# Batched A·Bᵀ in fp32: products in column halves, stores of pairs in 16 KB runs, and one fixed order of transfers on the sync queue

## The chip, the cores and the metric

One core of one Trainium2 chip. The metric is the device time of one execution in microseconds, taken as the median of several runs. Each run has a state. All runs quoted here were in the fast state, and fast runs alone are compared. In each batch of experiments the kernel before ran on the same chip as well. Its medians over the batches were 124.9 to 125.2 us, so ratios are worth more here than differences between medians of different batches. A difference of two ratios is called shown below only where their 95% intervals are clear of each other.

## The reference

```python
batch, m, k, n = 16, 512, 512, 512          # a: [16, 512, 512], b: [16, 512, 512], fp32
def reference(a, b):
    return np.matmul(a, b.transpose(0, 2, 1)).astype(np.float32)
```

33.55 MB are read and 16.78 MB are written. The kernel casts to bf16 and accumulates in fp32.

## The kernel before

The matrices are taken in pairs, u = 0 to 7. A load brings two matrices (2 MiB, 16 KB per partition) into one of seven slots. VectorE casts them to bf16, TensorE transposes them against an identity, ScalarE and VectorE copy the transposed slices out of PSUM, TensorE multiplies, and ScalarE moves the products into one of seven output slots. These are the parts that the change touches (cuts marked):

```python
load(0, nc.scalar)                      # loads: ScalarE's queue (one on the sync queue)
load(1, nc.sync)
for n in range(2, NL): load(n, nc.scalar)
...
nc.sync.wait_ge(s_ld[0], 32)            # stores: the sync queue, after the eighth load
for n in range(batch - 1): store(n)     # 1 MiB, 8 KB per partition
...
for u in range(pairs):                  # ScalarE, unrolled
    for ko in range(KO):
        nc.scalar.wait_ge(s_ta, KO * u + ko + 1)
        for e in range(2):              # two copies of 128x512, sorted by matrix
            c = nc.scalar.copy(out=ta[:, ko, ...], in_=tp[:, ko % 2, ...])
        c.then_inc(s_ea, 1)
    for n in (2 * u + NL, 2 * u + NL + 1):
        if n < 2 * pairs: load(n, nc.scalar)
    ...                                 # 8 copies ob <- ps
...
for e in range(2):                      # TensorE: matrix e of the pair
    ...
    t = nc.tensor.matmul(ps[:, j, :],
            ta[:, ko, (e * J + j) * P:(e * J + j + 1) * P],      # 128 columns
            tb[:, ko, :]...[:, :, e * HP:(e + 1) * HP], ...)     # 512 columns stream
```

Of the kernel before, what the change touches and what calls it, by code (L numbers as in the profile page):

```python
# [10 lines left out]
def kernel(  # L11
# [6 lines left out]
    nc = tc.nc  # L18
    P = 128
    batch, M, K = a.shape  # L20
    _, N, _ = b.shape
    J = M // P
    KO = K // P
    HP = P // 2
    HK = K // 2
    pairs = batch // 2
    f32 = mybir.dt.float32
    bf16 = mybir.dt.bfloat16
    NL = 7
    NO = 7  # L30



    def sbuf(name, shape, dtype):
        return ctx.enter_context(nc.sbuf_tensor(name, shape, dtype))

    def sem(name):
        return tc.alloc_semaphore(name)

    with tc.tile_critical(no_gpsimd_drain=True):  # L40
# [5 lines left out]
        )  # L46
        ta = sbuf("ta", [P, KO, 2 * J * P], bf16)
        tb = sbuf("tb", [P, KO, 2 * J * P], bf16)
        ob = sbuf("ob", [P, NO, J, N], f32)
        tp = ctx.enter_context(nc.psum_tensor("tp", [P, 4, 2 * J, P], bf16))  # L50
        ps = ctx.enter_context(nc.psum_tensor("ps", [P, 4, N], f32))

        s_set = sem("s_set")
        s_ld = [sem(f"s_ld{i}") for i in range(NL)]
        s_st = [sem(f"s_st{i}") for i in range(NO)]

        s_go = sem("s_go")
        s_wa = sem("s_wa")
        s_wb = sem("s_wb")
        s_ca = sem("s_ca")  # L60
# [2 lines left out]
        s_ta = sem("s_ta")  # L63
        s_tb = sem("s_tb")
        s_ea = sem("s_ea")
        s_eb = sem("s_eb")
        s_mm = sem("s_mm")
        s_pv = sem("s_pv")
        s_out = sem("s_out")
# [12 lines left out]
        def load(n, engine):  # L82
            u, slot = n // 2, n % NL
            src = (a if n % 2 == 0 else b)[2 * u:2 * u + 2].rearrange(
                "e (p j) k -> (e p) j k", j=2 * J
            )
            engine.dma_start(ld[:, slot], src).then_inc(s_ld[slot], 16)

        def landed(n):
            return s_st[n % NO], 16 * (n // NO + 1)  # L90

        def store(n):
            nc.sync.wait_ge(s_out, n + 1)
            nc.sync.dma_start(
                out[n].rearrange("(p j) n -> p j n", j=J), ob[:, n % NO]
            ).then_inc(landed(n)[0], 16)

        load(0, nc.scalar)
        load(1, nc.sync)
        for n in range(2, NL):  # L100
            load(n, nc.scalar)

        for n in range(2 * pairs):
            nc.gpsimd.wait_ge(s_ld[n % NL], 16 * (n // NL + 1)).then_inc(s_go, 1)  # L104

        nc.sync.wait_ge(s_ld[0], 32)
        for n in range(batch - 1):
            store(n)

        def taker(engine):  # L110
            return lambda s, n: engine.wait_ge(s, n).then_inc(s, -n)  # L111
# [5 lines left out]
        take = taker(nc.vector)  # L117
# [3 lines left out]
        with nc.Fori(0, pairs, engines=[dve]) as u:  # L121
            for x, (h, w, s_c, s_w) in enumerate(
                ((ha, wa, s_ca, s_wa), (hb, wb, s_cb, s_wb))
            ):
                src = ld[:, bass.ds((u * 2 + x) % NL, 1)].rearrange("p o j k -> p (o j) k")
                take(s_go, 1)
                if x == 0:
                    take(s_da, 1)

                nc.vector.tensor_copy(out=h[:, :J, :], in_=src[:, :J, :HK])  # L130
                nc.vector.tensor_copy(  # L131
                    out=h[:, J:, :], in_=src[:, J:, :HK]
                ).then_inc(s_c, 1)
                nc.vector.tensor_copy(out=w[:], in_=src[:, :, HK:]).then_inc(s_w, 1)  # L134
            for ko in range(KO):
                if ko == 0:
                    take(s_wa, 1)
                    take(s_da, 1)
                    nc.vector.tensor_copy(out=ha[:], in_=wa[:]).then_inc(s_ca, 1)  # L139
                take(s_tb, 1)  # L140
                if ko == 1:
                    take(s_wb, 1)
                    nc.vector.tensor_copy(out=hb[:], in_=wb[:]).then_inc(s_cb, 1)  # L143
                nc.vector.tensor_copy(  # L144
                    out=tb[:, ko, :],
                    in_=tp[:, 2 + ko % 2].rearrange("k j p -> k (j p)"),
                ).then_inc(s_eb, 1)


        act = nc.scalar.engine  # L150
        nc.scalar.nop().then_inc(s_ea, 2)
        nc.scalar.copy(out=one[:], in_=nc.const_aps.tensor(1.0, (P, 1), f32))  # L152
        for u in range(pairs):
            for ko in range(KO):
                nc.scalar.wait_ge(s_ta, KO * u + ko + 1)
                for e in range(2):
                    c = nc.scalar.copy(  # L157
                        out=ta[:, ko, e * J * P:(e + 1) * J * P].rearrange(
                            "k (j p h) -> k j p h", j=J, h=2
                        ),  # L160
                        in_=tp[:, ko % 2, :, e * HP:(e + 1) * HP].rearrange(
                            "k (h j) p -> k j p h", h=2
                        ),
                    )
                c.then_inc(s_ea, 1)


            for n in (2 * u + NL, 2 * u + NL + 1):
                if n < 2 * pairs:
                    load(n, nc.scalar)  # L170
            for e in range(2):
                n = 2 * u + e
                if n >= NO:
                    nc.scalar.wait_ge(*landed(n - NO))
                for j in range(J):
                    nc.scalar.wait_ge(s_mm, J * n + j + 1)
                    c = nc.scalar.copy(  # L177
                        out=ob[:, n % NO, j, :].rearrange("m (p j) -> m p j", j=2 * J),
                        in_=ps[:, j, :].rearrange("m (j p) -> m p j", j=2 * J),
                    )  # L180
                    if e == 0:
                        c.then_inc(s_pv, 1)
                    elif j in (0, J - 1):
                        c.then_inc(s_out, 1)
# [3 lines left out]
        take = taker(nc.tensor)  # L188
        with nc.Fori(0, pairs, engines=[pe]):
            with nc.Fori(0, 2, engines=[pe]):  # L190

                for x, (h, s_c, s_t, s_e) in enumerate(
                    ((ha, s_ca, s_ta, s_ea), (hb, s_cb, s_tb, s_eb))
                ):
                    take(s_c, 1)
                    for g in range(2):
                        take(s_e, 1)
                        for j in range(2 * J):
                            t = nc.tensor.transpose(  # L199
                                tp[:, 2 * x + g, j, :], h[:, j, g * P:(g + 1) * P], ident[:]  # L200
                            )
                            if x == 1 and g == 0 and j == 0:
                                t.then_inc(s_da, 1)
                        t.then_inc(s_t, 1)



            for e in range(2):
                for jj in range(0, J, 2):
                    if e == 1:  # L210
                        take(s_pv, 2)
                    for kk in range(0, KO, 2):
                        for j in (jj, jj + 1):
                            for ko in (kk, kk + 1):
                                if (e, jj, j) == (0, 0, 0) and ko >= 2:
                                    nc.tensor.wait_ge(s_ea, ko - 1)
                                    nc.tensor.wait_ge(s_eb, ko - 1)
                                t = nc.tensor.matmul(  # L218
                                    ps[:, j, :],
                                    ta[:, ko, (e * J + j) * P:(e * J + j + 1) * P],  # L220
                                    tb[:, ko, :].rearrange("k (j p) -> k j p", j=2 * J)[
                                        :, :, e * HP:(e + 1) * HP
                                    ],
                                    start=(ko == 0),
                                    stop=(ko == KO - 1),
                                )
                            if kk == KO - 2:
                                t.then_inc(s_mm, 1)



    with tc.tile_critical(sync_engine=act, no_gpsimd_drain=True):
        for n in range(batch - NO, batch - 1):
            nc.scalar.wait_ge(*landed(n))
    waits = nc.cur_bb.bb.instructions[-1]
    last = nc.sync.dma_start(
        out[batch - 1].rearrange("(p j) n -> p j n", j=J), ob[:, (batch - 1) % NO]
    )
    tc.add_manual_dep(
        last.ins,  # L240
        waits.name,
# [33 lines left out]
```

## Time and profile before

| | before |
|---|---|
| median (fast runs) | 124.92 us |
| span of the profiled run | 123.1 us |
| TensorE, VectorE, ScalarE busy | 73%, 55%, 55% |
| two transfer queues, share of 16 engines' span | 60.6% + 36.4% |
| last load used, last product stored from PSUM | 100.41 us, 113.80 us |

The lines behind this table, and what follows from them, stand in the prediction below.

One more reading is used in this document. Each transfer leaves 16 completion records in the trace, which I read as one from each of the 16 DMA engines. I took their times from the trace, counted from the start of the span. For the last load of the kernel before the first of them stands at 98.61 us and the last at 100.07 us. The first cast that needs it starts at 100.41 us. A load is usable when the slowest engine has finished it, and the kernel ends when the slowest engine has finished the last store: first record 120.56 us, last 122.08 us.

### The profile page before, as it was taken

What the parts mean: (1) busy time and instruction counts of PE and PEld (TensorE: products, weight loads), DVE (VectorE), ACT (ScalarE), POOL (GpSimd) and SP (SyncE); (2) the same over time, 40 slices, a digit from 0 to 9 for tenths busy, and PEclk for the clock granted to TensorE, in tenths of its full rate; (3) what the DMA queues carried; (4) which work ended last, traced back from release to release, by engine and by line L of the source; (5) the groups of instructions that cost most, each with busy time, mean ns of one, the idle gap of its engine ahead of it and who ended that gap; (6) DMA issues with size and microseconds to landing.
All of it is one profiled execution on the core that took longest, in us unless ns stands there. A gap on an engine that the chain in (4) does not pass through costs nothing. (4 is left out here: it accounts for less than half of the span.)

```text
span 123.1 us, 2235 instructions
## 1 busy us (share of the span) xinstructions
PE 90.1 (73%) x768; PEld 54.7 (44%) x768; DVE 67.9 (55%) x96; ACT 67.9 (55%) x130; POOL 0.7 (1%) x6
## 2 busy tenths in 40 slices
PE   0000089999999899989998999999699936997000
PEld 0000078447734764575477447644564425542000
DVE  0000598992896589388918983871987039600000
ACT  0400064567945966696589468855865184666000
POOL 2000000000000000000000000000000000000000
PEclk9999999999999999999999999999999999999965
DMA  4999999999999998999999999999999999999991
GB/s 144 394 426 431 447 437 431 426 431 426 426 431 426 426 405 373 453 399 437 407 429 426 463 405 442 437 415 434 423 418 458 399 426 423 431 429 423 426 431 45
DMA packets 4610, 50.34 MB, mean 409 GB/s; under 512 B 513, under 2 KB 513, under 8 KB 513
## 3 DMA queue, kind: packets, MB, share of 16 engines
q10 hardware_dynamic: 2160, 31.46, 60.6%
q1 hardware_dynamic: 2448, 18.88, 36.4%
q14 instruction: 2, 0.01, 0.0%
HBM read 33.55 MB, written 16.78 MB: 409 GB/s over the span
## 5 line engine op out<-in xcount | busy, mean ns | idle before, releaser
L218 PE MATMUL ps<-tb,ta 128*128 128x512 bf16 x256 | 57.8, 379 | 0.5
L177 ACT COPY ob<-ps 128x512 f32<-128x512 f32 x64 | 34.3, 590 | 26.3 <-PE ps L218 22.5
L157 ACT COPY ta<-tp 128x512 bf16<-128x512 bf16 x64 | 33.0, 613 | 15.5 <-PE tp L199 15.0
L218 PEld LDWEIGHTS ps<-tb,ta 128*128 128x128 bf16 x256 | 24.1, 98 | 30.6 <-issue 4.0
L199 PE MATMUL tp<-ident,ha 128*128 128x128 bf16 x256 | 18.5, 224 | 18.8 <-PEq L111 18.3
L199 PEld LDWEIGHTS tp<-ident,ha 128*128 128x128 bf16 x256 | 15.8, 100 | 22.3 <-issue 20.6
L144 DVE COPY tb<-tp 128x1024 bf16<-128x1024 bf16 x32 | 21.2, 685 | 3.6 <-DVEq L111 3.6
L199 PE MATMUL tp<-ident,hb 128*128 128x128 bf16 x256 | 17.5, 223 | 3.8 <-PEq L111 3.5
L199 PEld LDWEIGHTS tp<-ident,hb 128*128 128x128 bf16 x256 | 15.3, 100 | 5.0 <-issue 4.8
L130 DVE CAST ha<-ld 128x1024 bf16 x8 | 5.5, 690 | 14.6 <-POOLq L104 13.8
L139 DVE COPY ha<-wa 128x2048 bf16<-128x2048 bf16 x8 | 5.5, 691 | 12.4 <-DVEq L111 12.4
L130 DVE CAST hb<-ld 128x1024 bf16 x8 | 5.5, 689 | 8.4 <-DVEq L111 8.4
L134 DVE CAST wa<-ld 128x2048 bf16 x8 | 9.8, 1220 | 0.0
L134 DVE CAST wb<-ld 128x2048 bf16 x8 | 9.8, 1220 | 0.0
L131 DVE CAST hb<-ld 128x1024 bf16 x8 | 5.5, 687 | 0.0
L131 DVE CAST ha<-ld 128x1024 bf16 x8 | 5.5, 687 | 0.0
L143 DVE COPY hb<-wb 128x2048 bf16<-128x2048 bf16 x8 | 5.5, 684 | 0.0
L152 ACT ACT_TABLE_LOAD x1 | 1.3, 1283 | 4.1 <-issue 4.1
L74 POOL TENSOR_SCALAR_AFFINE_SELECT ident<-ident 128x128 bf16<-128x128 bf16 x1 | 0.3, 292 | 0.2 <-POOL ident L72 0.2
L72 POOL MEMSET ident<- 128x128 bf16 x1 | 0.2, 204 | 0.5 <-SPq L40 0.5
L152 ACT COPY one<-const-float32-1.0 128x1 f32<-128x1 f32 x1 | 0.2, 191 | 0.0
L259 POOL MEMSET const-bfloat16-1.0<- 128x1 bf16 x1 | 0.1, 102 | 0.0
(3 smaller groups left out, 0.3 us busy)
## 6 DMA issues: line engine op xcount, KB each, us to landing
ld<-in_a_dram ACTq DMA_DIRECT2D x8, 2048.0 KB, 29.3
out_dram<-ob SPq DMA_DIRECT2D x16, 1024.0 KB, 25.6
ld<-in_b_dram ACTq DMA_DIRECT2D x7, 2048.0 KB, 27.1
ld<-in_b_dram SPq DMA_DIRECT2D x1, 2048.0 KB, 12.6
```

Source lines behind the costliest of these rows:

```text
L74: nc.gpsimd.affine_select(out=ident[:], in_=ident[:], compare_op=mybir.AluOpType.not_equal, fill=1.0, base=0, pattern=[[-1, P]], channel_m ...
L130: nc.vector.tensor_copy(out=h[:, :J, :], in_=src[:, :J, :HK])
L131: nc.vector.tensor_copy(out=h[:, J:, :], in_=src[:, J:, :HK]).then_inc(s_c, 1)
L134: nc.vector.tensor_copy(out=w[:], in_=src[:, :, HK:]).then_inc(s_w, 1)
L139: nc.vector.tensor_copy(out=ha[:], in_=wa[:]).then_inc(s_ca, 1)
L143: nc.vector.tensor_copy(out=hb[:], in_=wb[:]).then_inc(s_cb, 1)
L144: nc.vector.tensor_copy(out=tb[:, ko, :], in_=tp[:, 2 + ko % 2].rearrange("k j p -> k (j p)"),).then_inc(s_eb, 1)
L152: nc.scalar.copy(out=one[:], in_=nc.const_aps.tensor(1.0, (P, 1), f32))
L157: c = nc.scalar.copy(out=ta[:, ko, e * J * P:(e + 1) * J * P].rearrange("k (j p h) -> k j p h", j=J, h=2), in_=tp[:, ko % 2, :, e * HP:(e ...
L177: c = nc.scalar.copy(out=ob[:, n % NO, j, :].rearrange("m (p j) -> m p j", j=2 * J), in_=ps[:, j, :].rearrange("m (j p) -> m p j", j=2 * J),)
L199: t = nc.tensor.transpose(tp[:, 2 * x + g, j, :], h[:, j, g * P:(g + 1) * P], ident[:])
L218: t = nc.tensor.matmul(ps[:, j, :], ta[:, ko, (e * J + j) * P:(e * J + j + 1) * P], tb[:, ko, :].rearrange("k (j p) -> k j p", j=2 * J)[:, ...
```

## The change

The intent: with 64-column products the two matrices of a pair land in the lower and the upper half of the PSUM partitions. An output partition then holds eight consecutive rows of one matrix, which is 16 KB in one run, and a pair can be stored as one transfer of 2 MiB. All transfers but the first are issued from the sync queue in one fixed order, so that no load can be overtaken in an unplanned way. ScalarE no longer issues loads and becomes a loop. The core of the diff:

```diff
-        load(0, nc.scalar); load(1, nc.sync); for n in range(2, NL): load(n, nc.scalar)
-        for n in range(batch - 1): store(n)
+        order = [("L", n) for n in range(9)]
+        for n, halves in enumerate(STORES[:-1]):          # 6 pairs, 4 single halves
+            order.append(("S", n))
+            if halves[-1] % 2: ...                         # then two more loads
+        for what, n in order:
+            if what == "L":
+                if n >= NL: nc.sync.wait_ge(s_cd, n - NL + 2)
+                load(n, nc.scalar if n == 0 else nc.sync)
+            else:
+                nc.sync.wait_ge(s_out, STORES[n][-1] + 1)
+                store(n).then_inc(landed(n)[0], 16)
 ...
-                for e in range(2): c = nc.scalar.copy(out=ta[...128x512...], ...)
+                nc.scalar.copy(out=ta[:, ko, :], in_=tp[:, ko % 2]...)      # 128x1024
 ...
-                                t = nc.tensor.matmul(ps[:, j, :], ta[... 128 columns], ...)
+                            for e in range(2):
+                                half = slice(e * HP, (e + 1) * HP)
+                                t = nc.tensor.matmul(ps[half, j % 4, :],
+                                    ta[:, ko, j * P + e * HP:j * P + (e + 1) * HP], ...)
```

The resulting order is: loads 0 to 8, store of pair 0, loads 9 and 10, store of pair 1, loads 11 and 12, store of pair 2, loads 13 and 14, stores of halves 6 and 7, load 15, then the stores that are left.

More of the change, by code (lines that the diff above doesn't have):

```diff
@@ L29 @@
     NL = 7
+    W = 2 * J
     NO = 7
+    NS = 5
+    STORES = []
+    for u in range(pairs):
+        if 2 * u % NO == NO - 1 or u == pairs - 1:
+            STORES += [(2 * u,), (2 * u + 1,)]
+        else:
+            STORES += [(2 * u, 2 * u + 1)]
+    OF = {h: n for n, halves in enumerate(STORES) for h in halves}
     def sbuf(name, shape, dtype):
@@ L48 @@
         tb = sbuf("tb", [P, KO, 2 * J * P], bf16)
-        ob = sbuf("ob", [P, NO, J, N], f32)
+        ob = sbuf("ob", [P, NO * J, N], f32)
         tp = ctx.enter_context(nc.psum_tensor("tp", [P, 4, 2 * J, P], bf16))
@@ L54 @@
         s_ld = [sem(f"s_ld{i}") for i in range(NL)]
-        s_st = [sem(f"s_st{i}") for i in range(NO)]
+        s_st = [sem(f"s_st{i}") for i in range(NS)]
         s_go = sem("s_go")
+        s_of = sem("s_of")
+        s_cd = sem("s_cd")
         s_wa = sem("s_wa")
@@ L89, in landed @@
         def landed(n):
-            return s_st[n % NO], 16 * (n // NO + 1)
+            return s_st[n % NS], 16 * (n // NS + 1)
         def store(n):
-            nc.sync.wait_ge(s_out, n + 1)
-            nc.sync.dma_start(
-                out[n].rearrange("(p j) n -> p j n", j=J), ob[:, n % NO]
-            ).then_inc(landed(n)[0], 16)
-        load(0, nc.scalar)
-        load(1, nc.sync)
-        for n in range(2, NL):
-            load(n, nc.scalar)
-        for n in range(2 * pairs):
-            nc.gpsimd.wait_ge(s_ld[n % NL], 16 * (n // NL + 1)).then_inc(s_go, 1)
-        nc.sync.wait_ge(s_ld[0], 32)
-        for n in range(batch - 1):
-            store(n)
+            halves = STORES[n]
+            u, lo = halves[0] // 2, halves[0] % 2 * J
+            at = halves[0] % NO * J
+            return nc.sync.dma_start(
+                out[2 * u:2 * u + 2].rearrange("e (p w) n -> (e p) w n", w=W)[
+                    :, lo:lo + len(halves) * J, :
+                ],
+                ob[:, at:at + len(halves) * J],
+            )
+        order = [("L", n) for n in range(9)]
+        nl = 9
+        for n, halves in enumerate(STORES[:-1]):
+            order.append(("S", n))
+            if halves[-1] % 2:
+                for _ in range(2):
+                    if nl < 2 * pairs:
+                        order.append(("L", nl))
+                        nl += 1
+        for what, n in order:
+            if what == "L":
+                if n >= NL:
+                    nc.sync.wait_ge(s_cd, n - NL + 2)
+                load(n, nc.scalar if n == 0 else nc.sync)
+                nc.gpsimd.wait_ge(s_ld[n % NL], 16 * (n // NL + 1)).then_inc(s_go, 1)
+            else:
+                nc.sync.wait_ge(s_out, STORES[n][-1] + 1)
+                store(n).then_inc(landed(n)[0], 16)
+                if n <= OF[2 * pairs - 1 - NO]:
+                    nc.gpsimd.wait_ge(*landed(n)).then_inc(s_of, len(STORES[n]))
         def taker(engine):
@@ L128 @@
                     take(s_da, 1)
-                nc.vector.tensor_copy(out=h[:, :J, :], in_=src[:, :J, :HK])
+                nc.vector.tensor_copy(
+                    out=h[:, :J, :], in_=src[:, :J, :HK]
+                ).then_inc(s_cd, 1)
                 nc.vector.tensor_copy(
@@ L150 @@
         act = nc.scalar.engine
+        take = taker(nc.scalar)
         nc.scalar.nop().then_inc(s_ea, 2)
+        nc.scalar.nop().then_inc(s_of, NO)
         nc.scalar.copy(out=one[:], in_=nc.const_aps.tensor(1.0, (P, 1), f32))
-        for u in range(pairs):
+        with nc.Fori(0, pairs, engines=[act]) as u:
             for ko in range(KO):
-                nc.scalar.wait_ge(s_ta, KO * u + ko + 1)
-                for e in range(2):
-                    c = nc.scalar.copy(
-                        out=ta[:, ko, e * J * P:(e + 1) * J * P].rearrange(
-                            "k (j p h) -> k j p h", j=J, h=2
-                        ),
-                        in_=tp[:, ko % 2, :, e * HP:(e + 1) * HP].rearrange(
-                            "k (h j) p -> k j p h", h=2
-                        ),
-                    )
-                c.then_inc(s_ea, 1)
-            for n in (2 * u + NL, 2 * u + NL + 1):
-                if n < 2 * pairs:
-                    load(n, nc.scalar)
-            for e in range(2):
-                n = 2 * u + e
-                if n >= NO:
-                    nc.scalar.wait_ge(*landed(n - NO))
-                for j in range(J):
-                    nc.scalar.wait_ge(s_mm, J * n + j + 1)
-                    c = nc.scalar.copy(
-                        out=ob[:, n % NO, j, :].rearrange("m (p j) -> m p j", j=2 * J),
-                        in_=ps[:, j, :].rearrange("m (j p) -> m p j", j=2 * J),
-                    )
-                    if e == 0:
@@ new lines @@
+                if ko < KO - 1:
+                    nc.scalar.wait_ge(s_ta, ko + 1)
+                else:
+                    take(s_ta, KO)
+                nc.scalar.copy(
+                    out=ta[:, ko, :], in_=tp[:, ko % 2].rearrange("k j p -> k (j p)")
+                ).then_inc(s_ea, 1)
+            for i in range(2):
+                take(s_of, 1)
+                dst = ob[:].rearrange("m (h j) n -> m h j n", j=J)[
+                    :, bass.ds((u * 2 + i) % NO, 1)
+                ].rearrange("m o j n -> m (o j) n")
+                for j in range(J):
+                    if (i, j) != (1, J - 1):
+                        nc.scalar.wait_ge(s_mm, i * J + j + 1)
+                    else:
+                        take(s_mm, W)
+                    c = nc.scalar.copy(
+                        out=dst[:, j, :].rearrange("m (p j) -> m p j", j=W),
+                        in_=ps[:, j, :].rearrange("m (j p) -> m p j", j=W),
+                    )
+                    if i == 0:
@@ L204 @@
                         t.then_inc(s_t, 1)
-            for e in range(2):
-                for jj in range(0, J, 2):
-                    if e == 1:
-                        take(s_pv, 2)
-                    for kk in range(0, KO, 2):
-                        for j in (jj, jj + 1):
-                            for ko in (kk, kk + 1):
-                                if (e, jj, j) == (0, 0, 0) and ko >= 2:
-                                    nc.tensor.wait_ge(s_ea, ko - 1)
-                                    nc.tensor.wait_ge(s_eb, ko - 1)
-                                t = nc.tensor.matmul(
-                                    ps[:, j, :],
-                                    ta[:, ko, (e * J + j) * P:(e * J + j + 1) * P],
-                                    tb[:, ko, :].rearrange("k (j p) -> k j p", j=2 * J)[
-                                        :, :, e * HP:(e + 1) * HP
-                                    ],
+            for jj in range(0, W, 2):
+                if jj >= J:
+                    take(s_pv, 2)
+                for kk in range(0, KO, 2):
+                    for j in (jj, jj + 1):
+                        for ko in (kk, kk + 1):
+                            if j == 0 and ko >= 2:
+                                nc.tensor.wait_ge(s_ea, ko - 1)
+                                nc.tensor.wait_ge(s_eb, ko - 1)
+                            for e in range(2):
+                                half = slice(e * HP, (e + 1) * HP)
+                                t = nc.tensor.matmul(
+                                    ps[half, j % 4, :],
+                                    ta[:, ko, j * P + e * HP:j * P + (e + 1) * HP],
+                                    tb[:, ko, :].rearrange("k (j p) -> k j p", j=W)[:, :, half],
                                     start=(ko == 0),
@@ L226 @@
                                 )
-                            if kk == KO - 2:
-                                t.then_inc(s_mm, 1)
+                        if kk == KO - 2:
+                            t.then_inc(s_mm, 1)
     with tc.tile_critical(sync_engine=act, no_gpsimd_drain=True):
-        for n in range(batch - NO, batch - 1):
+        for n in range(len(STORES) - 1 - NS, len(STORES) - 1):
             nc.scalar.wait_ge(*landed(n))
     waits = nc.cur_bb.bb.instructions[-1]
-    last = nc.sync.dma_start(
-        out[batch - 1].rearrange("(p j) n -> p j n", j=J), ob[:, (batch - 1) % NO]
-    )
+    last = store(len(STORES) - 1)
     tc.add_manual_dep(
```

## The prediction

> **What bounds the kernel now.** I read the page from the top: busy shares, then the slices, then the queues. The second fence of this part comes from a table of stretches that I asked for afterwards, and the third from the timeline.
>
> ```profile
> PE 90.1 (73%) x768; PEld 54.7 (44%) x768; DVE 67.9 (55%) x96; ACT 67.9 (55%) x130; POOL 0.7 (1%) x6
> ...
> DMA  4999999999999998999999999999999999999991
> ...
> DMA packets 4610, 50.34 MB, mean 409 GB/s; under 512 B 513, under 2 KB 513, under 8 KB 513
> ...
> q10 hardware_dynamic: 2160, 31.46, 60.6%
> q1 hardware_dynamic: 2448, 18.88, 36.4%
> ...
> PE 6%; ACT 0%; ACTq 0%; issue 0%
> ```
>
> The reader is to see that no engine is busy all the time (TensorE 73%, the others 55% or less), while the row of the DMA engines reads 9 in all slices but the first, one in the middle and the last. The two queues together fill 60.6 + 36.4 = 97.0% of sixteen engines' span. The chain that ended last holds only some 7% of the span, so by itself it explains nothing: the kernel moves a fixed 50.34 MB, and this fills the time from about 1.8 us to about 120.2 us of a span of 123.1 us. The median of 124.9 us has another 1.8 us outside the span.
>
> The columns of the next rows are the stretch, its length, the busy time of each engine with its instruction count, the granted clock, the DMA share and GB/s.
>
> ```profile
> 4.00:42.00 38.00, 25.43 (x224) 16.52 (x224) 22.22 (x31) 19.18 (x37) 0.00 (x0) 1.00 1.01 429
> 42.00:46.00 4.00, 3.56 (x40) 2.37 (x39) 3.55 (x7) 3.01 (x6) 0.00 (x0) 1.00 1.04 410
> 46.00:100.00 54.00, 50.87 (x427) 30.15 (x425) 36.03 (x51) 36.58 (x71) 0.00 (x0) 1.00 1.00 425
> 100.00:119.00 19.00, 10.23 (x80) 5.70 (x80) 6.12 (x9) 9.16 (x18) 0.00 (x0) 0.98 1.01 426
> ```
>
> Until 42 us there are only loads (the first store is issued at 42.75 us, because the store queue waits for the eighth load), from 46 to 100 us loads and stores are mixed from two queues, and after 100 us there are only stores. The rate is 429, 425 and 426 GB/s. It is nearly flat, and this is the most important fact for the prediction: whatever the mixture, the transfers run at almost one rate.
>
> The third view is the rhythm of the computation where nothing held it up, from the timeline:
>
> ```profile
> 44.51 7.29 PE L218 MATMUL ps<-tb,ta 128*128 128x512 bf16 x32
> ...
> 51.63 1.06 PE L199 MATMUL tp<-ident,ha 128*128 128x128 bf16 x16
> ...
> 55.97 7.29 PE L218 MATMUL ps<-tb,ta 128*128 128x512 bf16 x32
> ...
> 98.80 2.05 ACT L177 COPY ob<-ps 128x512 f32<-128x512 f32 x4 [3.07 <-DMA out_dram<-ob]
> ...
> 100.41 0.69 DVE L130 CAST hb<-ld 128x1024 bf16 x1 [4.77 <-DVEq L111]
> ...
> 112.73 1.07 ACT L177 COPY ob<-ps 128x512 f32<-128x512 f32 x2 [0.60 <-PE ps L218]
> ```
>
> One pair of matrices costs 55.97 - 44.51 = 11.46 us of TensorE's time: 7.29 us for 32 products (about 222 ns each) and 4.17 us for its transposes with their waits. A pair moves 6 MiB = 6.29 MB, which at 426 GB/s is 14.77 us. So computation has 3.3 us of slack per pair. The last load is used at 100.41 us, the last result is ready at 113.80 us, and stores that are still queued keep the DMA engines full until about 120 us. That is some 6 us of slack at the tail.
>
> [...] one load queue before 42 us gives 429 GB/s, two queues after 46 us give 425. [...]
>
> **The change, part by part.**
>
> Bytes. Loads stay 16 of 2 MiB. The 16 stores of 1 MiB become 10: six pairs of 2 MiB and four of 1 MiB (the ring of seven halves wraps once, and the last pair is split). 50.34 MB stay 50.34 MB. A transfer now has 128 + 16 records as before (2160 / 15 = 144), so the records should go from 4610 to 26 x 144 + 2 = 3746.
>
> Longer runs. Does a 16 KB run cost less per byte than an 8 KB run? The load queue took 60.6% of 16 x 123.1 us = 1193.6 us for 31.46 MB, which is 37.94 us per MB of one engine's time, all in 16 KB runs. The other queue took 36.4%, or 716.9 us, for 18.88 MB. Without its one load (2.10 MB x 37.94 = 79.7 us) its 8 KB stores cost 637.2 / 16.78 = 37.97 us per MB. The difference of 0.03 us per MB, on the 12.6 MB that get longer runs, over 16 engines, is 0.02 us. By this measure the longer runs are worth nothing. The stores-only stretch (426 against 429) says up to 0.7%, or 0.007 x 12.6 MB / 426 GB/s = 0.2 us. I book 0.1 us.
>
> One fixed order on one queue. This takes away the mixing of two queues. If all stretches ran at the 429 of loads alone, 42 to 46 us would shrink by 4 x 19 / 429 = 0.18 us, 46 to 100 us by 54 x 4 / 429 = 0.50 us, and 100 to 119 us by 19 x 3 / 429 = 0.13 us: 0.81 us in all. The last term is a stores-only rate that an order does not change. I book 0.5 us of the other 0.68.
>
> Can the one queue run dry? At 426 GB/s a 2 MiB unit takes 4.92 us from a start at 2.0 us. In the fixed order the ninth load ends at 46.3 us, the first store at 51.2, the last load at 100.4, and the five stores after it at 105.3, 110.2, 115.2, 117.6 and 120.1 us. Each item must be issued before its turn. The first store needs pair 0, done near 27 us, and its turn is at 46.3. The eleventh load needs the cast of the third pair, whose first load lands at 26.6 us, and its turn is at 56.1. The last load needs a cast near 57 us, turn 95.5. The last stores need halves 14 and 15. With the last load at 100.4 us, as before, these should be ready near 111.7 and 113.8 us, and their turns are at 115.2 and 117.6 us. So no turn is missed, by 3.5 us at the closest. ScalarE's wait for the last ring slot ends when the store of pair 4 lands near 107 us, before that half is evicted from about 110 us. Cost: 0.
>
> Column halves. 256 products of 128 columns become 512 of 64, each still streaming 512 columns. If the two halves of a pair run at the same time, 32 pairs take about 7.3 us as now. The weight loads double in number at half the width[...]. [...] Path: 0.
>
> ScalarE. Two copies of 128x512 (1.09 us for two in the timeline) become one of 128x1024, about 1.05 us, and the 64 evictions stay. Perhaps 1 us of 67.9 goes[...]. ScalarE also stops issuing loads. It is not on the path. Path: 0.
>
> Sum: 124.9 - 0.5 - 0.1 = 124.3 us.
>
> **The rivals.** First, the halves do not overlap. Then the products of a pair cost 64 x 222 ns = 14.2 us, with the transposes 18.4 us, over the 14.77 us of the transfers. TensorE, which starts at 15.4 us, would end at 15.4 + 8 x 18.4 = 163 us, and with the last store and the end of the kernel this makes about 170 us. For it: the trace has no column tile. [...] The overlap need not be full: up to 14.77 - 4.17 = 10.6 us for the products, a factor of only 1.35 over serial, hides. I give it 6%.
>
> Second, the order stalls. One store that waits for its result holds every load behind it, where two queues let loads pass. For it: the store queue waited 63.6 us for ScalarE before, which was harmless there. Against it: the turns above. A miss at one point would cost some us, perhaps 127 to 129 us. I give it 5%.
>
> Third, a larger gain: [...]
>
> Fourth, nothing: the transfers are at their rate and the order is a wash, 124.9 us.
>
> **Range and chances.** [...] 123.0 to 125.6 us. Faster by over 2% means under 122.5 us[...]: 4%. Slower by over 2% means over 127.4 us, from the first two rivals: 9%. The rest, 87%, is within 2%.
>
> **What would show it.** The DMA row should stay at 9, with the queues at about 4% and 92 to 93%, and 3746 records. The stretch from 46 to 100 us should read 427 to 430 GB/s in place of 425. The 64-column products should come in pairs with starts some ns apart and 32 pairs in about 7.3 us. If the burst takes 14 us, the first rival holds. If the DMA row shows a hole, the second does, and the sync queue's waits name the store. If the stores-only end reads above 430, the longer runs are worth more than I booked. A changed start or end of the transfers by more than 0.5 us would be a term that I do not have.

## The result and the profile after

| | before | after |
|---|---|---|
| median of 4 fast runs | 124.92 us | 126.41 us |
| ratio | 1 | 1.0117 (95% interval 1.0100 to 1.0135) |
| last load: first record, last record | 98.61, 100.07 us | 101.08, 103.85 us |
| last store: first record, last record | 120.56, 122.08 us | 122.88, 123.75 us |

A ratio is the mean time of one kernel's fast runs over that of the other's of the same rounds (in the experiments below without the profiled run of each), so it is not quite the ratio of the medians. The change made the kernel 1.2% slower. I had predicted 124.3 us with a range of 123.0 to 125.6 us.

First the page of the changed kernel: the row of the DMA engines in 40 slices, the packets, the queues (packets, MB, share of 16 engines), and the two groups of the new products (count, busy us, mean ns, idle before):

```profile
DMA  4999999999999999999999999999999999999493
...
DMA packets 3745, 50.35 MB, mean 404 GB/s; under 512 B 416, under 2 KB 416, under 8 KB 416
...
q1 hardware_dynamic: 3600, 48.24, 91.9%
q10 hardware_dynamic: 144, 2.10, 4.3%
q8 instruction: 1, 0.02, 0.0%
...
L248 PE MATMUL ps<-tb,ta 128*64 128x512 bf16 x512 | 57.7, 380 | 0.0
...
L248 PEld LDWEIGHTS ps<-tb,ta 128*64 128x64 bf16 x512 | 32.7, 110 | 22.0 <-issue 3.1
```

Two things are new. The DMA row has a 4 near the end, where it read 9 before. And there is a queue, q8, with one "instruction" packet of 16 KB. The page of before lists none of that size, only 0.01 MB on another queue, q14 (one packet of 8 KB at 48.8 us and one of 32 bytes at 0.1 us). The 512 narrow products need 57.7 us, as the 256 wide ones did (57.8 us): the halves do run side by side.

The same table of stretches as in the prediction, with the end cut finer:

```profile
4.00:42.00 38.00, 25.53 (x286) 18.45 (x287) 22.01 (x31) 17.04 (x25) 0.00 (x0) 1.00 1.00 429
42.00:46.00 4.00, 3.67 (x48) 2.48 (x46) 3.55 (x7) 2.97 (x4) 0.00 (x0) 1.00 1.08 369
46.00:100.00 54.00, 50.06 (x550) 35.05 (x550) 36.16 (x51) 34.43 (x52) 0.00 (x0) 0.97 1.00 425
100.00:116.00 16.00, 12.71 (x133) 8.89 (x130) 6.21 (x9) 8.10 (x12) 0.00 (x0) 0.89 0.97 415
116.00:119.00 3.00, 2.08 (x20) 0.88 (x16) 0.00 (x0) 2.17 (x4) 0.00 (x0) 1.00 0.63 262
119.00:123.00 4.00, 0.00 (x0) 0.00 (x0) 0.00 (x0) 0.00 (x0) 0.00 (x0) 0.77 0.89 369
```

From 46 to 100 us the rate is 425 GB/s, exactly as before: one order and longer runs gained nothing there. From 42 to 46 us it is 369 where it was 410. From 116 to 119 us it is 262: the transfers, which filled the span before, have a hole. I call the fall at 42 to 48 us the dip and the one at 116 to 119 us the hole.

The timeline of the end of the changed kernel shows what was late:

```profile
104.19 0.69 DVE L159 CAST hb<-ld 128x1024 bf16 x1 [5.84 <-DVEq L140]
...
107.52 1.86 PE L227 MATMUL tp<-ident,ha 128*128 128x128 bf16 x16 [0.69 <-PEq L140]
...
109.18 1.88 PE L227 MATMUL tp<-ident,hb 128*128 128x128 bf16 x16
...
110.99 7.10 PE L248 MATMUL ps<-tb,ta 128*64 128x512 bf16 x64
...
117.78 1.09 ACT L205 COPY ob<-ps 128x512 f32 x2 [0.60 <-PE ps L248]
```

and these are the same transposes in the kernel before:

```profile
103.74 1.05 PE L199 MATMUL tp<-ident,ha 128*128 128x128 bf16 x16 [0.68 <-PEq L111]
...
104.94 1.06 PE L199 MATMUL tp<-ident,hb 128*128 128x128 bf16 x16
```

The last load was usable 3.8 us later (104.19 against 100.41). The computation behind it took 118.87 - 104.19 = 14.7 us against 113.80 - 100.41 = 13.4 us, because two groups of transposes ran at 1.86 and 1.88 us in place of 1.05 and 1.06; the granted clock from 108 to 112 us was 0.64 there and 1.00 before. So the last store could only be issued near 119 us. At this point the loss looks explained: a late load, an exposed tail. The first experiment was made to test that, and it showed that this is not the whole story.

### The profile page after: what moved, and what is told of

Its sections match the earlier page's. It is cut to its first block, busy times and chain, and to the rows that moved or that the text cites. A ratio compares the mean times of both kernels' runs of the same rounds, so it can differ in the third digit from the quotient of the medians.

```text
span 124.7 us, 2826 instructions
## 1 busy us (share of the span) xinstructions
PE 94.0 (75%) x1024; PEld 65.8 (53%) x1024; DVE 67.9 (54%) x96; ACT 66.2 (53%) x98; POOL 0.7 (1%) x6
## 3 DMA queue, kind: packets, MB, share of 16 engines
q1 hardware_dynamic: 3600, 48.24, 91.9%
## 5 line engine op out<-in xcount | busy, mean ns | idle before, releaser
L248 PE MATMUL ps<-tb,ta 128*64 128x512 bf16 x512 | 57.7, 380 | 0.0
L205 ACT COPY ob<-ps 128x512 f32 x64 | 34.5, 588 | 27.2 <-PE ps L248 27.2
L248 PEld LDWEIGHTS ps<-tb,ta 128*64 128x64 bf16 x512 | 32.7, 110 | 22.0 <-issue 3.1
L192 ACT COPY ta<-tp 128x1024 bf16<-128x1024 bf16 x32 | 30.9, 1019 | 24.1 <-PE tp L227 24.1
L227 PE MATMUL tp<-ident,ha 128*128 128x128 bf16 x256 | 19.7, 235 | 18.0 <-PEq L140 18.0
L227 PEld LDWEIGHTS tp<-ident,ha 128*128 128x128 bf16 x256 | 16.6, 106 | 22.4 <-issue 21.9
L227 PE MATMUL tp<-ident,hb 128*128 128x128 bf16 x256 | 19.0, 234 | 6.0 <-PEq L140 5.6
L227 PEld LDWEIGHTS tp<-ident,hb 128*128 128x128 bf16 x256 | 16.8, 105 | 7.4 <-issue 7.4
```

Of the source, the lines that this page charges most:

```text
L192: nc.scalar.copy(out=ta[:, ko, :], in_=tp[:, ko % 2].rearrange("k j p -> k (j p)")).then_inc(s_ea, 1)
L205: c = nc.scalar.copy(out=dst[:, j, :].rearrange("m (p j) -> m p j", j=W), in_=ps[:, j, :].rearrange("m (j p) -> m p j", j=W),)
L227: t = nc.tensor.transpose(tp[:, 2 * x + g, j, :], h[:, j, g * P:(g + 1) * P], ident[:])
L248: t = nc.tensor.matmul(ps[half, j % 4, :], ta[:, ko, j * P + e * HP:j * P + (e + 1) * HP], tb[:, ko, :].rearrange("k (j p) -> k j p", j=W) ...
```

## The experiments

I held two theories at first. **Tail**: the last load is late, and computation and the last store behind it are exposed. **Lagging engine**: the mean DMA engine has a hole, but the slowest one has none, and since its bytes are the same in any order it sets the end. What spoke for the second is in the completion records of the changed kernel: the store of pair 6 was completed by the slowest engine at 118.80 us, the next one (1 MiB) at 121.27, and the last one (1 MiB) at 123.75, so 2.47 us for each, with no hole, while the first engine waited. A third theory put the loss on the **column halves** themselves.

### First batch: one part at a time

**The last load moved ahead of the stores of halves 6 and 7.**

```diff
-                for _ in range(2):
+                for _ in range(3 if n == 2 else 2):
```

> The changed kernel with one step of the order moved: the last load goes ahead of the stores of halves 6 and 7 instead of behind them. Theory tail (the last load came late, and computation and the last store behind it are exposed): the last load is used near 99 to 101 us instead of 104.19, TensorE's last product ends by 115.5 us, the hole at 116 to 119 us (262 GB/s) fills, and the time falls to 124.8 to 125.4 us. Rival, lagging engine (the slowest of the 16 DMA engines is busy without a hole up to the end, and its bytes are the same in any order): the hole fills for the mean, but the last landing stays near 123.7 us and the time at 126.2 to 126.6 us.

Measured: 126.20 us, ratio 1.0096 (1.0073 to 1.0119). Of its timeline, the cast of the last load and the last copy out of PSUM:

```profile
98.79 0.69 DVE L159 CAST hb<-ld 128x1024 bf16 x1
...
113.93 1.09 ACT L205 COPY ob<-ps 128x512 f32 x2 [0.60 <-PE ps L248]
```

and its table of stretches:

```profile
116.00:119.00 3.00, 0.00 (x0) 0.00 (x0) 0.00 (x0) 0.00 (x0) 0.00 (x0) 0.96 0.99 421
119.00:123.00 4.00, 0.00 (x0) 0.00 (x0) 0.00 (x0) 0.00 (x0) 0.00 (x0) 0.50 0.41 174
```

The load came 5.4 us earlier, the computation ended at 115.0 instead of 118.9 us, and the hole is gone (421 GB/s). But the gain is within the noise: 1.0096 against 1.0117, and 1.0100 when the changed kernel was run again. In the second line the DMA share falls to 0.41: some engines have finished and others have not. The first engine completed the last store at 120.46 us, as in the kernel before (120.56), and the slowest at 123.20 us (before: 122.08). The tail theory alone falls.

**The columns alone**, with the two queues and 1 MiB stores of before:

```diff
 # the kernel before, with the products, the copy ta <- tp and the output view of the changed one
-                for e in range(2): c = nc.scalar.copy(out=ta[...], in_=tp[...])
+                nc.scalar.copy(out=ta[:, ko, :], in_=tp[:, ko % 2]...).then_inc(s_ea, 1)
-                out[n].rearrange("(p j) n -> p j n", j=J)
+                out[2u:2u + 2].rearrange("e (p w) n -> (e p) w n", w=W)[:, n % 2 * J:n % 2 * J + J, :]
```

> The kernel before with only the computation changed: column halves, one ScalarE copy per transposed slice, stores of one half in 8 KB runs, the two queues and the unrolled ScalarE as before. Theory order (the loss comes from the queue and order): 124.7 to 125.2 us, and the product burst of a pair stays at 7.2 to 7.3 us. Rival, column halves cost time [...]: 125.8 us or more.

Measured: 125.27 us, ratio 1.0019 (0.9997 to 1.0042), last record at 122.43 us. The column halves cost about 0.2% here, 0.4% at most.

**The order alone**, with the 128-column products of before:

```diff
-        load(0, nc.scalar); load(1, nc.sync); for n in range(2, NL): load(n, nc.scalar)
+        # L0..L8, then S S L L, S S L L, ... all on nc.sync but L0, with the waits of the changed kernel
```

> The kernel before with only the order changed: all transfers but the first on the sync queue in the fixed order, the computation, the layout and the stores of 1 MiB as before. Theory order: 125.8 to 126.8 us, the last load used at 103 us or later, the DMA row with a dip near 116 to 119 us. Rival, column halves or the ScalarE loop cost the time: 124.7 to 125.2 us.

Measured: 127.02 us, just above the expected range, ratio 1.0149 (1.0118 to 1.0181). The last load was used at 105.70 us, and the slowest engine ended 3.6 us behind the first on it. The computation is that of before, so the loss is in the queue and the order.

**The pairs in another order**, to see what the dip at 44 to 48 us belongs to:

```diff
-            u, slot = n // 2, n % NL
+            u, slot = [0, 4, 1, 2, 3, 5, 6, 7][n // 2], n % NL      # and the same in store()
```

> The changed kernel with the pairs taken in the order 0, 4, 1, 2, 3, 5, 6, 7, nothing else. Both kernels show a dip of the transfers at 44 to 48 us, while the first matrix of the second half of the input is loaded. If the dip belongs to the addresses, it moves to 12 to 22 us and the stretch 42 to 48 us reads 420 to 430 GB/s; time within 0.5 us of 126.4. If it belongs to the moment (the first store coming up in the queue), it stays at 44 to 48 us.

Measured: 126.64 us, ratio 1.0138 (1.0106 to 1.0170). The dip stayed: the slice of its page at 43.5 to 46.6 us reads 348 GB/s. It does not belong to the addresses.

### Second batch: queues, runs, turns

**Paired stores, but two queues.**

```diff
-                load(n, nc.scalar if n == 0 else nc.sync)      # one order on the sync queue
+        # loads on ScalarE's queue at the places of the kernel before (ScalarE unrolled), stores on the sync queue
```

> The changed kernel with its column halves and its paired stores in 16 KB runs, but loads on the ScalarE queue and stores on the sync queue at the places of the kernel before, ScalarE unrolled for that. Theory one queue (the loss is in putting loads and stores through one queue[...]): 124.6 to 125.3 us, the last landing near 122.1 to 122.5 us. Rival, the paired stores or the column halves lose the time: 126 us or more.

This expectation missed widely. Measured: 135.46 us, ratio 1.0802 (1.0727 to 1.0877). The row of GB/s in 40 slices of 3.34 us, and the cast of the last load:

```profile
GB/s 137 417 431 431 431 431 431 431 431 417 441 422 431 358 407 451 402 446 419 441 417 446 417 431 429 426 439 441 417 446 412 446 417 446 201 0 0 0 404 223
```

```profile
114.06 0.69 DVE L151 CAST hb<-ld 128x1024 bf16 x1 [7.36 <-DVEq L132]
```

The rate is full until 114 us; then come three empty slices. The bytes were moved in the wrong order. The completion records say how (first records, us):

```text
                        loads 9, 10, 11           stores beside them
columns only (8 KB)     54.45  61.82  69.13       53.81  61.21  68.55   (1 MiB each)
paired stores (16 KB)   57.30  67.02  76.75       56.05  65.73  75.49   (2 MiB each)
```

With 8 KB runs a load of 2 MiB passes beside a store of 1 MiB every 7.3 us; with 16 KB runs beside a store of 2 MiB every 9.7 us. The run with paired stores holds a check of its own: the two halves 6 and 7 are stored singly, in 8 KB runs, and beside them loads 12 and 13 passed in 7.3 us each again (first records at 84.06 and 91.37 us). Loads are in 16 KB runs in both. So in bytes the loads got two for each one of the stores with 8 KB stores, and one for one with 16 KB stores: in these two runs the shares went with the run lengths. How the queues divide the engines was not shown. The loads lose, the last one lands at 113.7 us, and nothing is left to store while the last pair is computed. The kernel before owes its good order to its 8 KB stores. This is also why the changed kernel needs a fixed order: with two free queues paired stores cost 8%.

**Short runs in the one queue** (the changed kernel, every store a single half):

```diff
-            STORES += [(2 * u, 2 * u + 1)]
+            STORES += [(2 * u,), (2 * u + 1,)]           # for all pairs
```

> The changed kernel with all 16 stores of one half (1 MiB, 8 KB runs), still on one queue in the same order. By the prediction's sum the run length is worth 0.1 us, so 126.4 to 126.6 us. The order-only run, which had 8 KB runs too, suggests that the long runs repair a part of what the one queue costs: then 126.8 to 127.4 us, with a lower rate from 52 to 100 us than the changed kernel.

Measured: 126.63 us, ratio 1.0129 (1.0098 to 1.0159). This is not distinguishable from the changed kernel, so within one queue the run length is worth nothing that can be measured here.

**The same with alternating order** (store, load, store, load):

```diff
-            if halves[-1] % 2:
-                for _ in range(2): ...two loads
+            if nl < 2 * pairs: ...one load after each store
```

> The short-run kernel with its order changed from store, store, load, load to store, load, store, load: twice as many turns between writing and reading in the one queue, same bytes, same queue. Theory turns (each change of direction stalls some engines): 0.5 us or more above the short-run kernel, and more long packets. Rival, the turns are free and the queue alone matters: within 0.3 us of the short-run kernel.

Measured: 125.96 us, ratio 1.0080 (1.0046 to 1.0115). It is not slower, rather faster, so neither expectation was met. Changes between writing and reading did not each cost time here (1.0080 with twice as many, against 1.0129), and the theory of turns falls. In this order 39 MiB are moved up to and with the last load, as in the kernel before, not 40: the first record of that load is at 98.66 us (before: 98.61) and no hole is left at the end. The slowest engine still ended at 123.13 us.

**The first store two loads earlier.**

```diff
-        order = [("L", n) for n in range(9)]
+        order = [("L", n) for n in range(7)]             # rest shifted, last load at the same place
```

> The changed kernel with the first store moved from behind the ninth load to behind the seventh (the later order is shifted so that the last load has the same bytes ahead). If the dip of the transfers at 44 to 47 us belongs to the first turn from loads to stores, it moves to 34 to 37 us and 42 to 48 us reads 420 GB/s or more. If it belongs to the time since the start, or to the ninth load, it stays at 44 to 47 us. Time near 126.4 us in both.

Measured: 127.02 us, ratio 1.0159 (1.0112 to 1.0206). Its stretches:

```profile
33.00:37.00 4.00, 4.00 (x41) 2.38 (x40) 3.80 (x6) 2.00 (x4) 0.00 (x0) 1.00 0.97 299
42.00:48.00 6.00, 5.67 (x69) 3.87 (x68) 5.54 (x9) 4.27 (x6) 0.00 (x0) 1.00 1.01 431
```

The dip moved with the first store: 299 GB/s at 33 to 37 us, where the changed kernel has 422, and 431 at 42 to 48 us, where the changed kernel has 352. In the changed kernel it comes while the last load ahead of the first store is moving: that load's records stand at 47.46 to 48.80 us, those of the load before it at 41.76 to 42.67. The time was expected near 126.4 us; its interval overlaps that of the changed kernel, so the 0.4% above it stay unexplained.

### Third batch: can the dip be paid early?

**A 64 KB store of zeros at the start**, overwritten later by the true result, in the kernel before, in the changed one and in the alternating one:

```diff
+        nc.sync.wait_ge(s_bl, 1)
+        nc.sync.dma_start(out[0].rearrange("(p j) n -> p j n", j=J)[:, 0, :128], blank[:]).then_inc(s_first, 16)
```

> The kernel before with one added transfer: a 64 KB store of zeros into the first output matrix right behind the second load, overwritten by the true result later. Theory first store (the dip at 44 to 47 us is the price of the first store of the program): the dip moves to the first few us and shrinks because little is in flight then, 42 to 48 us reads 420 GB/s or more, and the time falls by 0.2 to 0.6 us, to about 99.6% of the kernel before. Rival, the dip is the price of the first full-size turn from loads to stores: it stays at 44 to 47 us and the time is unchanged or 0.2 us longer.

> The changed kernel with the same small early store. Theory first store: the dip at 44 to 47 us, which cost 0.9 us of the mean engine here against 0.5 us in the kernel before, is gone and the time falls to 125.4 to 125.9 us; what is left above the kernel before is lagging engines and the exposed tail. Rival: 126.3 to 126.7 us with the dip in its place.

> The alternating one-queue kernel (short runs, store, load, store, load) with the small early store: no exposed tail and no dip. Theory first store: 0.4 to 0.8 us under the alternating kernel, 125.1 to 125.6 us, so within 0.4% of the kernel before, the rest being the lagging engine. Rival: 125.9 to 126.3 us.

Measured: ratios 1.0014 (0.9998 to 1.0030), 1.0105 (1.0087 to 1.0122) and 1.0081 (1.0060 to 1.0102). The dip stayed in all three; in the first:

```profile
42.00:48.00 6.00, 5.55 (x59) 3.57 (x57) 5.46 (x9) 4.75 (x10) 0.00 (x0) 1.00 1.00 395
```

against 393 in this stretch of the kernel before. (In the same stretch the other two have 377 and 340 GB/s.) So it goes with the first full-size turn from loads to stores, not with the first store of the program. Why that turn stalls, and why later ones hardly do (425 GB/s from 46 to 100 us), stays open.

**The changed kernel again**, in the same rounds:

> The changed kernel unaltered, to stand beside the two others in the same rounds: 126.2 to 126.6 us, ratio 1.010 to 1.0135, dip at 44 to 47 us and hole at 116 to 119 us in place, and one 16 KB instruction packet near 53 us again.

Measured: 126.30 us, ratio 1.0100 (1.0079 to 1.0121). The last load's records are at 101.06 and 103.85 us, as in the first profile. The hole is shallower: 382 GB/s from 116 to 119 us.

### Fourth batch: one queue or one instruction packet?

The page of each kernel with column halves lists one instruction packet of 16 KB. At 53.0 us of the changed kernel it held one DMA engine for 932 ns; a data packet of that size took 611 ns in the median. On the store that was ending then, the slowest engine was 1.11 us behind the first; on load 9, the next transfer, it was 1.92 us behind.

**Full columns, alternating order, one queue:**

```diff
 # the order-only kernel
-            order += [("S", 2 * u), ("S", 2 * u + 1)]   # then two loads
+            # S, L, S, L
```

> The kernel before with all transfers but the first on one queue, in the alternating order (store, load, store, load) instead of the order-only run's store, store, load, load; full 128-column products, no ScalarE loop. If the loss belongs to the one queue alone: ratio 1.006 to 1.010 like the alternating kernel with column halves. If a part of it belongs to the 16 KB instruction packet that all kernels with column halves show near 53 us: 1.003 to 1.006, no such packet, and no single engine that falls back by 1 us while the tenth load lands.

Measured: 126.13 us, ratio 1.0080 (1.0049 to 1.0110), and no such packet on its page. One queue in a good order costs 0.5 to 1.1% even without column halves.

**The same with TensorE's inner loop written out:**

```diff
-            with nc.Fori(0, 2, engines=[pe]):
+            for _ in range(2):
```

> The run above with TensorE's inner loop of two passes of transposes written out twice: the same work in the same order, but as many TensorE instructions in the program as with column halves (96 transposes and products a pair in place of 64). If the 16 KB instruction packet near 53 us comes from the length of TensorE's program, it appears here, one DMA engine falls back by about 0.6 to 1 us at that moment, and the time is 0.2 to 0.6 us above the run above. Else no packet and the same time.

The packet appeared (of the queues of this run's page):

```profile
q8 instruction: 1, 0.02, 0.1%
```

It started at 31.2 us, held an engine for 1078 ns, and the slowest engine went from 0.73 us behind the first on load 4 to 1.68 us on load 5, which was in flight at that moment. The second slowest only went from 0.62 to 0.74 us, and both stayed where they were up to load 7. So the packet does come with the longer TensorE program, and at that moment one engine falls back by almost 1 us. The 1078 ns are what the packet took from one engine here. In the time it is not resolved: 126.38 us, ratio 1.0094 (1.0071 to 1.0117), against 1.0080 without the packet. On the last store the slowest engine was 2.22 us behind the first without the packet and 2.31 us with it, so little of that 1 us is left there.

**The columns-only kernel and the alternating one again**, in these rounds:

> The columns-only kernel again (two queues, short runs), in the same rounds: ratio 1.000 to 1.004, with the 16 KB instruction packet but the last landing near 122.4 us.

> The alternating one-queue kernel with column halves again: ratio 1.006 to 1.010. Against the columns-only kernel it differs in the one queue, its order and the ScalarE loop alone, so the difference of the two ratios is what the one queue costs where no tail is exposed: 0.5 to 0.8%.

Measured: 125.51 us, ratio 1.0028 (1.0006 to 1.0051), and 126.11 us, ratio 1.0068 (1.0045 to 1.0091). Their difference, 0.4% or 0.5 us, is what the one queue (with its order and the ScalarE loop) costs where no tail is exposed. That is under the expected 0.5 to 0.8%, and the two intervals overlap slightly (1.0051 against 1.0045). With full columns, where nothing but the queue and the order differ from the kernel before, the same cost is 0.8% (1.0049 to 1.0110) and clear of zero.

The records of all kernels without a hole, side by side:

```text
                              last store: first record   last record   ratio
before (two queues)                       120.56           122.08      1
before, early 64 KB store                 120.76           122.18      1.0014
columns only (two queues)                 120.48           122.43      1.0019
columns only, again                       120.68           122.78      1.0028
one queue, full columns, alternating      120.70           122.92      1.0080
the same, long TensorE code               120.74           123.05      1.0094
one queue, halves, alternating            120.71           123.13      1.0080
one queue, last load first                120.46           123.20      1.0096
alternating, early 64 KB store            121.13           123.48      1.0081
alternating, again                        120.86           123.59      1.0068
```

The records are from one profiled execution each, the ratios from several timed ones, so single rows need not agree in order. The groups do: the fastest engine finishes within 0.7 us in all of them, the slowest at 122.1 to 122.8 us with two queues and at 122.9 to 123.6 us with one, and the ratios are 1.0000 to 1.0028 and 1.0068 to 1.0096. No version beat the kernel before.

## Why the prediction was wrong, point by point

**What bounds the kernel: right.** The transfers do; the change of the computation alone moved the time by 0.2 to 0.3%. But the prediction read the end of the transfers off the mean of the engines, about 120.2 us. The slowest of them had its last record at 122.08 us in that same trace.

**Bytes and packets: right.** 3744 packets of the transfers (26 x 144) and one of instructions, against the predicted 3746, and queue shares of 91.9% and 4.3% against some 92 to 93% and 4%.

**Column halves: right.** 64 narrow products took 7.10 to 7.23 us where 32 wide ones took 7.29, so the two halves overlap fully, a factor of two. The first rival fell (its limit of 10.6 us is a factor of 1.34, not 1.35, over serial). The narrower weight loads had no measured size before the change, so my zero for them was an estimate. Each took 110 ns in the mean for 64 columns, against 98 ns for 128. So they were not faster here for being narrower, but they stayed hidden (57.7 us of products against 57.8). From one group of products to the next TensorE took 11.60 us (44.81 to 56.41 us) against 11.46, still below the 14.77 us of the transfers. What I did not have is the longer TensorE program and its instruction packet.

**ScalarE: right.** A copy of 128x1024 took 1.02 us where I had put 1.05, and ScalarE was busy for 66.2 us in place of 67.9.

**Longer runs, booked at -0.1 us: too small to be seen.** Short and long runs in the one queue gave 1.0129 and 1.0117. The intervals reach 0.2 to 0.3% to each side, so the runs do not contradict 0.1 us and do not show it.

**One fixed order on one queue, booked at -0.5 us: this is the step that failed, in its sign.** I took the lower rate of the mixed stretch as the price of two queues. In one queue this stretch ran at the same 425 GB/s, so the 0.68 us were not there to be gained. In its place the one queue cost 0.4 to 0.8%, or 0.5 to 1.0 us, even in the kernels in which no turn was missed, and it cost it at the slowest engine. With the last load moved ahead, the first engine ended at 120.46 us, as before (120.56), and the slowest at 123.20 against 122.08. The time follows the slowest engine: in every trace of the table above the span ends 1.0 us after the last record. (My "one load queue before 42 us" was two up to 13.5 us, with load 1 on the sync queue; from 16 to 42 us the rate was 427 to 429 GB/s as well.) One queue and two nearly agreed in the rate from 46 to 100 us (421 to 424 GB/s in the one-queue kernels that have no hole, 425 to 426 with two), but not in the end of the slowest engine.

**"Can the one queue run dry? ... Cost: 0": wrong as well, but a small part of the loss.** I let the last load land at 100.4 us by dividing bytes by the mean rate. The first engine had it at 101.08 us (0.7 us later than the sum; the dip alone, estimated from its rate, is (429 - 352) x 6 / 429 = 1.1 us), the slowest 2.77 us after that, and the cast began at 104.19 us. My schedule had no spread at all: it ran 16 engines as one. On the first load the slowest engine was 0.93 us behind the first in the kernel before and 0.90 in the changed one, on the last load 1.45 and 2.77 us. That the kernel before also used its last load at 100.41 us was a coincidence, which I took for agreement ("as before"). There the load was the end of 39 MiB, first record at 98.61, and 1.45 us of spread followed; in the fixed order it is the end of 40 MiB, and one MiB takes 2.45 us. The alternating order, with 39 MiB, brought the first record back to 98.66. The computation behind the late load then took 1.3 us more at a lower clock (0.64 from 108 to 112 us, 1.00 before), so the last result was ready at 118.87 us and missed its announced turn, 117.6 us, by 1.3 us. But the run with the last load first missed no turn, filled the hole and still took 126.20 us: the missed turn is not where most of the 1.2% went.

**How the 1.2% divide** is not settled. In two queues the column halves cost 0.2 to 0.3% (not cleanly separated from zero in the first run, 1.0006 to 1.0051 in the second). In both runs the 16 KB instruction packet came near 53 us and the slowest engine ended 0.3 to 0.7 us later than before (122.43 and 122.78 us); whether the packet is the cause there was not tested. The one queue costs 0.4% on top of them (1.0068 against 1.0028 in the same rounds), but 0.8% without them (1.0080), so the two do not simply add. The rest, some 0.2 to 0.5%, goes with the order store, store, load, load. With column halves its interval overlaps that of the alternating order (1.0129 against 1.0080); with full columns it is clear of it, though the two runs are from different batches (1.0149, from 1.0118 up, against 1.0080, up to 1.0110). The single parts carry uncertainties of about 0.3% each. In the changed kernel the two limits, the tail and the slowest engine, end within half a microsecond or so of each other (123.75 and, in the second profile, 123.33 us, against 123.20 with the tail removed), which may be why removing the tail alone gained almost nothing.

**The rivals and the signs.** The second rival, a stall of the order, foretold the hole. I gave it 5%, and the sign for it, a hole in the DMA row, did appear, but filling the hole gained 0.04 to 0.2%. The 6% for the first rival was my estimate: no trace of before had two column halves side by side. The third rival, a larger gain, and the lower end of my range were estimates too, from an upper rate that was not shown. No rival named the spread of the engines. The sign that came true was the last one: the end of the transfers moved by more than 0.5 us (122.08 to 123.75 us), a term that I did not have.

**What stays open.** Why single engines fall back more in one queue than in two is not shown. Nor is the one queue separated from its serial order: no run issued the fixed order from two queues. The dip is deeper in one queue, too (340 to 380 GB/s over 42 to 48 us, 381 to 395 with two queues and 8 KB stores), and no run tells what that costs. What causes the dip at the first turn is open as well.

## What to carry to other kernels

When transfers fill the span, plan with the slowest of the DMA engines, not with the mean rate: a load is usable, and a kernel ended, when the last engine is done, and here this alone was worth 1.5 to 2.8 us. With two queues the run length of the stores set here how fast the loads beside them went (7.3 us a load with 8 KB runs, 9.7 us with 16 KB); change the run length and the order must be checked again. And before putting everything into one order, count the bytes ahead of the last load, because each MiB there took 2.45 us of the tail here. One queue was not free either: 0.4 to 0.8% here, at nearly the same mean rate (421 to 424 GB/s against 425 to 426).
